# A transformer layer on one core: global q statistics in pairs with four square places, ropes on VectorE, and a curved schedule for the modulation products

## The chip, the cores and the metric

The kernel runs on one core of a Trainium2 chip. The metric is the device time of one execution in microseconds; three executions of the kernel before were timed. The profile is one further execution, recorded by the hardware profiler.

## The reference

One layer of a hybrid diffusion backbone: 1024 latent tokens of width 1024, 256 context tokens, float32. What matters here is the projection stage:

```
mod   = silu(c) @ w_mod + b_mod            # 6 x 1024 values: shift, scale, gate of mixer and FFN
mod_c = silu(c_ctx) @ w_mod[:, :2*1024] + ...   # the two that the context tokens need
h     = x   * (1 + scale1)  + shift1
h_c   = ctx * (1 + mod_c[1]) + mod_c[0]
proj  = h @ w_in + b_in                    # qa, ka, va, qb, kb, vb, gate logits (2 x 1024)
q_a   = rope(qa)                           # 8 heads of 64, windowed attention
q_b   = rope(rms(qb) * q_norm_g)           # 8 heads of 64, global attention
rms(t) = t * rsqrt(mean(t*t over the head) + 1e-6)
gates = sigmoid(gate logits)               # weights of the two branches
```

Behind it come the two attentions, their merge with the gates, a layer norm, a ConvFFN and a second layer norm.

## The kernel before

**Products in three parts.** Each float32 operand is split into a high part (a copy rounded to `fp32r`, line L82) and a low part (the difference, L87). `mm3` multiplies two operands with three matmuls: high by high (L90), high by low (L91), low by high (L92). A weight tile 128 x 512 is fetched into a raw tile (`raw`, 3 of them), then split into a pair of `wp` tiles (8, that is 4 pairs). In names, `w` is the raw tile, `wh` the high part, made on ScalarE, `wl` the low part, made on VectorE for the q and kv weights and on GpSimd for the gate weights (`wlg`).

**Order of TensorE's work.** First the global q (`q1`, names `accq1`, weights `wqb` of `in_w_qb`): 8 k tiles of the contraction x 8 token tiles x 3 matmuls, with the sums in all eight PSUM banks. While it runs, the tokens are modulated into `hT` (`hh`, `hl`). Then the program goes through a written list, `order`, made from `GORD = 3, 4, 4, 1, 4`: 3 gate tiles, `qa` (8 steps k), 4 gates, `qb` (8 steps), 4 gates, `ka` (8 steps), 1 gate, `kb` (8 steps), 4 gates. Here `qa` and `qb` are the windowed branch's q for token tiles 0-3 and 4-7 (both with the weights of `in_w_qa`; the names `wqa`/`wqb`, `accqa`/`accqb` follow the group), and `ka`, `kb` are keys and values with the context tokens, `cx`. A gate tile has two halves of 24 matmuls each; a step of `qa` or `qb` has 12. The loads of each step are issued ahead by `prefetch`: 2 or 4 steps early, as the 8 `wp` tiles allow.

**Modulation products.** 48 columns of the modulation matrix are wanted beside this work (16 for the context, 32 for the latent tokens' other factors). The list `late` holds them, and `mods(us)` is called behind each step with the number of matmuls of it. Each product takes a slot of the rotation of 19 large tiles (`ht`, H0 to H18, 128 x 1024, first put back is first taken), fetches a row block `wml` of 512 KB on SP's queue (L650) and multiplies and sums it on VectorE (`mod`, L188). So the rate follows the TensorE work done: `span[0]/span[1]` is the share of the matmuls up to the end of `ka` (840) that has been issued, and before the change the number of products issued is that share of 48:

```
        for _ in range(min(int(total * span[0] / span[1] + 0.01) - n, len(late))):
```

The slot is put back at once, so the next user of it waits for the product. The tiles `Q` (pairs of token tiles of a q) and the gates `sg` (until `late` is empty) take slots of the same rotation.

**The queue of side work.** `queue` holds for every token tile the steps behind its evacuation (`q_evac`, bias added while PSUM is read: VectorE, L301 for the global q, L299 for `qa`/`qb`). `side_step` takes one entry (in the slow mode every second time) and runs its first step; the remaining ones run at the next calls. For a global q tile, `qpost(1, t)` has a step `s1` (the rope table with the norm's gain folded in, by GpSimd; squares on ScalarE, L282, into one of two places `sqq`; sum per head on VectorE, L285; scaling and eps on VectorE, L286; power -1/2 on GpSimd, L287; the negative on GpSimd), an empty step, and `s2`: the rope (`rope`, L263 to L271: a product with the cosines, two half products with the sines, a sum), which goes to GpSimd for t = 2 and 5 and to VectorE else. The result of `s1` is read in attention. For `qa` and `qb` tiles `qpost(0, t)` holds only a rope.

**What sets the order.** Every engine and every DMA queue carries out its instructions in the order of the program. SP issues nearly all loads, so a load whose tile is not free holds the loads behind it. ScalarE's stream holds the high parts of the weights, the squares, the scaling of the context tiles `cx` (L632/L633, which need modulation columns 0 to 15) and the sigmoids of the gates with the issue of their stores (L668/L669); VectorE's holds the low parts, products, evacuations, statistics and ropes.

Of the kernel before, what the change touches and what calls it, by code (L numbers as in the profile page):

```python
# [7 lines left out]
F32 = mybir.dt.float32  # L8
R32 = mybir.dt.float32r
AF = mybir.ActivationFunctionType  # L10
ALU = mybir.AluOpType
AX = mybir.AxisListType

P = 128
# [4 lines left out]
NT = 8  # L19
HD = 64  # L20
# [5 lines left out]
QK_EPS = 1e-6  # L26
# [36 lines left out]
VOFF = 0.0  # L63
VSPAN = 1.0
VSC = 0, 1
DNS = {u0 + 2 * n + (u0 == 20): (n, j0, j1) for u0, j0, j1 in ((16, 0, 4), (20, 4, 8), (24, 8, 11)) for n in range(3)}


@with_exitstack
def layer_kernel(  # L70
# [6 lines left out]
    nc = tc.nc  # L77
# [18 lines left out]
    def ctile(shape, dt, name):  # L96
        return const.tile(shape, dt, tag=name, name=name)
# [15 lines left out]
    pqs, nqs = (cvt[:, n * 64:n * 64 + 64].rearrange("p (a b) -> p a b", b=8) for n in (0, 1))  # L113
    onec = ctile([P, 1], F32, "onec")
    onesf = ctile([P, P], F32, "onesf")
    mhalf = ctile([P, 8], F32, "mhalf")
    nc.vector.memset(onec, 1.0)
    nc.vector.memset(onesf, 1.0)
    nc.vector.memset(mhalf, -0.5)
# [13 lines left out]
    def ht(name, shape=(P, T), dt=F32):  # L133
        hslot[name] = pool, tag = hfree.pop(0)
        return pool.tile(list(shape), dt, tag=tag, name=name, bufs=1)

    def hput(*names):
        for n in names:
            hfree.append(hslot.pop(n))
# [5 lines left out]
    ph1 = tc.alloc_tile_pool(name="ph1", bufs=1, side="right", reuse_waits="tile")  # L145
# [9 lines left out]
    def pw(name, shape=(P, 512), dt=F32):  # L155
        return ph1.tile(list(shape), dt, tag="pw", name=name, bufs=PWB)
# [10 lines left out]
    def bias_tile(src, nm):  # L167
        b = ph1.tile([P, 512], F32, tag="bias", name=nm, bufs=2)
        nc.sync.dma_start(b, src.partition_broadcast(P))
        return b  # L170
# [11 lines left out]
    def tmp(name):  # L182
        t = ht(name)
        hput(name)
        return t

    def mod(w, row, bias, o):
        nc.vector.tensor_tensor_reduce(out=w, in0=w, in1=row, scale=1.0, scalar=bias, op0=ALU.mult, op1=ALU.add,  # L188
                                       accum_out=o)

    hT = []
    Q = {}
# [64 lines left out]
    def bc(ap, H):  # L257
        return ap.unsqueeze(1).to_broadcast([P, H, HD])

    def rope(eng, dst, src, H, cs, sn, nm, t1=None, t2=None):  # L260
        if t1 is None:
            t1, t2 = pw(f"rt1{nm}"), pw(f"rt2{nm}")
        eng.tensor_tensor(out=t1.rearrange("p (h d) -> p h d", d=HD), in0=src.rearrange("p (h d) -> p h d", d=HD),  # L263
                          in1=bc(cs, H), op=ALU.mult)
        sv = src.rearrange("p (h r a f) -> p h r a f", r=2, a=2, f=16)
        tv = t2.rearrange("p (h r a f) -> p h r a f", r=2, a=2, f=16)
        sg = sn.rearrange("p (r a f) -> p r a f", r=2, a=2)
        for a in (0, 1):
            eng.tensor_tensor(out=tv[:, :, :, a, :], in0=sv[:, :, :, 1 - a, :],
                              in1=sg[:, :, a, :].unsqueeze(1).to_broadcast([P, H, 2, 16]), op=ALU.mult)  # L270
        eng.tensor_tensor(out=dst, in0=t1, in1=t2, op=ALU.add)  # L271

    def gfold(dst, gi, t, eng):
        eng.tensor_tensor(out=dst[:, 0], in0=ropec[:, t], in1=gcol[:, gi], op=ALU.mult)
        sv = ropes[:, t].rearrange("p (r a f) -> p r a f", r=2, a=2)
        gv = gcol[:, gi].rearrange("p (r a f) -> p r a f", r=2, a=2)
        dv = dst[:, 1].rearrange("p (r a f) -> p r a f", r=2, a=2)
        for a in (0, 1):
            eng.tensor_tensor(out=dv[:, :, a, :], in0=sv[:, :, a, :], in1=gv[:, :, 1 - a, :], op=ALU.mult)

    def rms_scale(x3, H, nm, sq, ss=None):
        nc.scalar.activation(sq.rearrange("p (h d) -> p h d", d=HD), x3, AF.Square)  # L282
        if ss is None:
            ss = ph1.tile([P, 8], F32, tag="ss", name=f"ss{nm}", bufs=4)[:, 0:H]
        nc.vector.tensor_reduce(out=ss, in_=sq.rearrange("p (h d) -> p h d", d=HD), axis=AX.X, op=ALU.add)  # L285
        nc.vector.tensor_scalar(out=ss, in0=ss, scalar1=1.0 / HD, scalar2=QK_EPS, op0=ALU.mult, op1=ALU.add)  # L286
        nc.gpsimd.tensor_tensor(out=ss, in0=ss, in1=mhalf[:, 0:H], op=ALU.pow)  # L287
        return ss
# [4 lines left out]
    def q_evac(br, t, acc, bias):  # L293
        if t % 2 == 0:
            Q[br, t] = ht(f"Q{br}_{t}", (P, 2, 512))
        qq = Q[br, t - t % 2]
        q = qq[:, t % 2]
        if br == 0:
            nc.vector.scalar_tensor_tensor(out=q, in0=acc, scalar=0.125, in1=bias, op0=ALU.mult, op1=ALU.add)  # L299
        else:  # L300
            nc.vector.tensor_tensor(out=q, in0=acc, in1=bias, op=ALU.add)  # L301

    def qtile(br, t):
        return Q[br, t - t % 2][:, t % 2]

    def qpost(br, t):
        q = qtile(br, t)
        q3 = q.rearrange("p (h d) -> p h d", d=HD)
        if br == 0:
            def r0():  # L310
                rope(nc.gpsimd if t % 3 == 2 else nc.vector, q, q, 8, ropec[:, t], ropes[:, t], f"q0_{t}")
            return [r0]
        st = {}

        def s1():
            st["tb"] = ph1.tile([P, 2, HD], F32, tag="tb", name=f"tbq{t}", bufs=4)
            gfold(st["tb"], 0, t, nc.gpsimd)
            rms_scale(q3, 8, f"q{t}", sqq[0][:, t % 2], pqs[:, t])
            if t == NT - 1:
                sqq.clear()  # L320
                hput("sqq")
            nc.gpsimd.tensor_scalar(out=nqs[:, t], in0=pqs[:, t], scalar1=-1.0, scalar2=0.0, op0=ALU.mult, op1=ALU.add)

        def s2():
            tb = st["tb"]
            rope(nc.gpsimd if t % 3 == 2 else nc.vector, q, q, 8, tb[:, 0], tb[:, 1], f"q1_{t}")
        return [s1] + [lambda: None] * GAP + [s2]

    sqq = [ht("sqq", (P, 2, 512))]
    bias_qb = bias_tile(b_qb, "bias_qb")  # L330
    for t in range(NT):
        q_evac(1, t, acc[t], bias_qb)

    KL, KC, VT = [], [], []

    def kv_alloc():
        KL.extend(ht(f"KL{h}", dt=R32) for h in range(4))
        KC.append(ht("KC", (P, 4, NC), R32))
        VT.extend(ht(f"VT{t}", (P, 2, 4, P), R32) for t in range(5))
# [249 lines left out]
    def wd_sums(n, j0, j1):  # L589
        def a(r, c):  # L590
            return w_dn[c * NH + j0:c * NH + j1][:, :, 4 * r:4 * r + 4].rearrange("n p f q -> p n (f q)")

        def put(key, src, *more):
            tag = tokens.pop()
            t = dpool.tile([P, j1 - j0, HALF], F32, tag=tag, name=f"sd{key}_{j0}")
            for j in range(j0, j1):
                sd[key, j] = t[:, j - j0]
            sd[key] = t
            nc.sync.dma_start(t, src)
            for m in more:  # L600
                nc.gpsimd.dma_start(t, m, accum_op=ALU.add)

        if n == 0:
            put(1, a(1, 0), a(1, 1))
            put(3, a(0, 0), a(1, 0))
        elif n == 1:
            put(2, sd[1], a(0, 0))
        else:
            put(4, sd[2], a(0, 1))
# [28 lines left out]
    late = [(col, scc, modx[:, col:col + 1]) for col in range(16)]  # L638
    late += [(col, sc, modc[:, col:col + 1]) for col in range(16, 48)]

    total = len(late)
    span = [0.0, 0.0]

    def mods(us):
        span[0] += us
        n = total - len(late)
        for _ in range(min(int(total * span[0] / span[1] + 0.01) - n, len(late))):
            col, row, o = late.pop(0)
            w = tmp(f"wml{len(late)}")
            nc.sync.dma_start(w, wmodT[col])  # L650
            mod(w, row, bmc[:, col:col + 1], o)
            if not late:
                hput("sc", "scc")
                kv_alloc()
# [46 lines left out]
    for n, (gi, k) in enumerate(order):  # L701
# [9 lines left out]
        nm, src, tiles = groups[gi]  # L711
# [4 lines left out]
        for t in tiles:  # L716
            if t < NT:
                s = slice(t * P, (t + 1) * P)
                a = hT[k][0][:, s], hT[k][1][:, s]
            else:  # L720
                s = slice((t - NT) * P, (t - NT + 1) * P)
                a = c[0][:, s], c[1][:, s]
            mm3(acc[t], a, w, k == 0, k == KT - 1)
        mods(3 * len(tiles))
        if k == KT - 1:
            for t in tiles:
# [106 lines left out]
    for u in range(nu + 1):  # L833
# [3 lines left out]
        ss = []  # L837
        if u < nu:
            ss = units[u].score_steps()
# [11 lines left out]
        if u < nu:  # L851
            ss = [units[u].context] + ss
# [4 lines left out]
        for _, st_ in sorted(seq, key=lambda e: e[0]):  # L857
            st_()
        if u in DNS:
            wd_sums(*DNS[u])  # L860
        if u < nu:
# [82 lines left out]
    for f in range(2, KT):  # L944
# [4 lines left out]
        for j in range(4):  # L949
            k = (f % 2) * 4 + j  # L950
            for hf in (0, 1):
                a = O[1, hf, 0, j // 2][:, j % 2], O[1, hf, 1, j // 2][:, j % 2]
# [234 lines left out]
    for f in (4, 6):  # L1187
        for si in (1, 2):
# [3 lines left out]
            elif f == 6:  # L1192
                second = ln1(2)
                a = [n for n in range(len(pend)) if len(pend) - n <= KT]
# [122 lines left out]
    for k in range(4):  # L1317
        steps = build(k)
        n = 2 if k < 2 else 0
# [234 lines left out]
    nm = post.tile([P, nt], F32, tag="bnm", name="bnm")  # L1554
# [58 lines left out]
    for n in OTO:  # L1613
        t, a = n
# [122 lines left out]
```

## Time and profile before

| | |
|---|---|
| median of 3 runs | 1587.97 us (1587.14 to 1588.69) |
| span of the profiled execution | 1585.4 us |
| own time of the profiled execution | not given beside its span |
| TensorE (PE) busy | 1528.4 us, 96% |
| VectorE (DVE) busy | 1195.6 us, 75% |
| ScalarE (ACT) busy | 813.0 us, 51% |
| GpSimd (POOL) busy | 753.7 us, 48% |

The profile's page lists the busy time of each engine, the span in 40 slices with the granted TensorE clock and the DMA traffic, the chain of work that ended last, and groups of instructions: line, engine, operation, output <- inputs, count, then busy time, mean of one in ns, and the idle time of the engine just ahead of them with what ended it. A timeline row gives start and length in us, engine, line, operation and tiles; in square brackets stands the idle time of the engine ahead of the instruction and who ended it, and `x4` at the end means four instructions in a row taken together. The stage that the change touches lies between 16 and 345 us of the span.

### The profile page before, as it was taken

What the parts mean: (1) busy time and instruction counts of PE and PEld (TensorE: products, weight loads), DVE (VectorE), ACT (ScalarE), POOL (GpSimd) and SP (SyncE); (2) the same over time, 40 slices, a digit from 0 to 9 for tenths busy, and PEclk for the clock granted to TensorE, in tenths of its full rate; (3) what the DMA queues carried; (4) which work ended last, traced back from release to release, by engine and by line L of the source; (5) the groups of instructions that cost most, each with busy time, mean ns of one, the idle gap of its engine ahead of it and who ended that gap; (6) DMA issues with size and microseconds to landing.
All of it is one profiled execution on the core that took longest, in us unless ns stands there. A gap on an engine that the chain in (4) does not pass through costs nothing.

```text
span 1585.4 us, 22064 instructions
## 1 busy us (share of the span) xinstructions
PE 1528.4 (96%) x7680; PEld 1269.8 (80%) x7680; DVE 1195.6 (75%) x1766; ACT 813.0 (51%) x1443; POOL 753.7 (48%) x731
## 2 busy tenths in 40 slices
PE   6999999999999999999999999999999999999996
PEld 5878788878887887777788898888888888888876
DVE  7797646628888777888674779888888877657886
ACT  5422222448887667688531565444444444435642
POOL 0574302426667556665422554666667764021132
PEclk9999999999999999999999999999999999999998
DMA  9695662322236555531451132333334446996721
GB/s 378 217 313 188 221 217 81 120 80 67 62 104 157 139 127 145 118 73 39 142 186 53 60 101 86 114 107 112 115 106 118 111 113 189 358 273 210 255 94 53
DMA packets 112367, 229.98 MB, mean 145 GB/s; under 512 B 12960, under 2 KB 27808, under 8 KB 112160
## 3 DMA queue, kind: packets, MB, share of 16 engines
q1 hardware_dynamic: 96816, 198.93, 37.6%
q0 software_dynamic: 10400, 20.19, 8.2%
q10 hardware_dynamic: 5040, 9.46, 1.6%
q8 instruction: 60, 0.98, 0.3%
q14 instruction: 51, 0.42, 0.1%
HBM read 177.35 MB, written 65.86 MB: 153 GB/s over the span
## 4 chain that ended last, share of the span: by engine, by line
PE 82%; DVE 6%; ACT 4%; issue 3%; POOL 2%; DMA 2%; ACTq 0%; SPq 0%; DVEq 0%; POOLq 0%
PE ptr L531 5%; PE p L90 4%; PE p L91 4%; PE p L92 4%; PE g L90 3%; PE g L91 3%; PE g L92 3%; PE b L92 3%; PE b L91 3%; PE b L90 3%; PE s L414 2%; PE a L92 2%; PE c L91 2%; PE d L91 2%; PE c L92 2%
## 5 line engine op out<-in xcount | busy, mean ns | idle before, releaser
L541 DVE TENSOR_TENSOR ptl<-ptr,pth 128x512 fp32r<-128x512 f32 x188 | 124.8, 685 | 27.5 <-ACT pth L540 25.2
L531 PE MATMUL ptr<-ident,p 128*128 128x128 f32 x816 | 126.5, 278 | 10.3 <-DVE ptl L541 7.8
L540 ACT CAST pth<-ptr 128x512 fp32r<-128x512 f32 x188 | 106.6, 588 | 56.3 <-PE ptr L531 32.7
L87 DVE TENSOR_TENSOR ld<-rd,hd 128x1024 fp32r<-128x1024 f32 x77 | 94.0, 1240 | 52.5 <-ACT hd L82 50.4
L426 ACT ACTIVATE p<-p,nm 128x1024 f32<-128x1024 f32 (+2 forms) x128 | 125.3, 981 | 10.9 <-DVE p L459 10.1
L531 PEld LDWEIGHTS ptr<-ident,p 128*128 128x128 f32 x816 | 93.8, 140 | 40.3 <-DVE ptl L541 13.5
L82 ACT CAST hd<-rd 128x1024 fp32r<-128x1024 f32 x77 | 79.2, 1050 | 81.5 <-PE p L92 50.0
L552 PE MATMUL av<-pth,VT 128*128 128x512 f32 x236 | 104.6, 443 | 1.0 <-ACT avs L558 0.5
L90 PE MATMUL p<-hd 128*128 128x512 f32 x264 | 103.2, 391 | 0.0
L92 PE MATMUL p<-hd,ld 128*128 128x512 f32 x264 | 102.7, 389 | 0.0
L91 PE MATMUL p<-ld,hd 128*128 128x512 f32 x264 | 102.7, 389 | 0.0
L90 PE MATMUL g<-hh,whg 128*128 128x512 f32 x256 | 99.9, 390 | 0.0
L92 PE MATMUL g<-hh,wlg 128*128 128x512 f32 x256 | 99.7, 389 | 0.0
L91 PE MATMUL g<-hl,whg 128*128 128x512 f32 x256 | 99.6, 389 | 0.0
L553 PE MATMUL av<-ptl,VT 128*128 128x512 f32 x236 | 97.6, 414 | 2.0 <-POOL ptl L87 1.9
L87 POOL TENSOR_TENSOR wlg<-wg,whg 128x512 fp32r<-128x512 f32 x32 | 47.0, 1479 | 109.6 <-ACT whg L82 107.3
L459 DVE TENSOR_SCALAR_CACHE_REDUCE p<-s,cvt,nmc 128x1024 f32<-128x1024 f32 x64 | 84.5, 1340 | 12.3 <-PE s L415 11.8
L414 PE MATMUL s<-KL,q 128*128 128x512 f32 (+2 forms) x192 | 76.0, 396 | 2.9 <-ACT p_x L426 2.0
L188 DVE CUSTOM_DVE_ANT_0 wml<-wml,sc,bmc 128x1024 f32<-128x1024 f32 x32 | 45.0, 1416 | 39.0 <-DMA wml<-in_wmodT_dram 38.6
L84 POOL TENSOR_SCALAR pth<-prw 128x512 fp32r<-128x512 f32 x48 | 31.1, 649 | 88.2 <-ACT prw L537 62.7
L82 ACT CAST wS<-s 128x512 fp32r<-128x512 f32 x76 | 45.3, 621 | 52.1 <-POOL s L1079 51.3
L415 PE MATMUL s<-KL,q 128*128 128x512 f32 (+2 forms) x192 | 71.7, 373 | 0.0
(396 smaller groups left out, 4974.0 us busy)
## 6 DMA issues: line engine op xcount, KB each, us to landing
wml<-in_wmodT_dram SPq DMA_DIRECT2D x48, 512.0 KB
ru<-in_w_up_dram SPq DMA_DIRECT2D x38, 512.0 KB
rd<-td SPq DMA_DIRECT2D x55, 256.0 KB
rd<-sd SPq DMA_DIRECT2D x44, 256.0 KB
rd<-in_w_dn_dram SPq DMA_DIRECT2D x33, 256.0 KB
wm<-in_wmodT_dram SPq DMA_DIRECT2D x16, 512.0 KB
wg<-in_w_g_dram SPq DMA_DIRECT2D x32, 256.0 KB
sgd<-sg ACTq DMA_DIRECT2D x32, 256.0 KB
```

What stands on the lines that cost most here:

```text
L82: nc.scalar.copy(hi, src)
L87: lo_eng.tensor_tensor(out=lo, in0=src, in1=hi.bitcast(F32), op=ALU.subtract)
L90: nc.tensor.matmul(ps, a[0], b[0], start=start, stop=False, skip_group_check=resumed)
L91: nc.tensor.matmul(ps, a[0], b[1], start=False, stop=False, skip_group_check=resumed)
L92: nc.tensor.matmul(ps, a[1], b[0], start=False, stop=stop, skip_group_check=resumed)
L414: nc.tensor.matmul(o, self.q[0][:, hs], ks, start=True, stop=False)
L426: nc.scalar.activation(p, s, AF.Exp, bias=nm[:, h:h + 1], scale=scale, accum_out=sm[:, h:h + 1])
L531: nc.tensor.transpose(tr[:, h * P:(h + 1) * P], self.pslice(h, n), ident)
L540: nc.scalar.copy(hi, tr)
L541: nc.vector.tensor_tensor(out=lo, in0=tr, in1=hi.bitcast(F32), op=ALU.subtract)
L552: nc.tensor.matmul(self.av, v, hi, start=first, stop=False)
L553: nc.tensor.matmul(self.av, v, lo, start=False, stop=self.left == 0)
```

## The change

- The squares of the global q have two tiles `sqq0`, `sqq1` of two places each instead of one such tile. One ScalarE instruction squares two token tiles (128 x 1024). The first two are issued beside the evacuation (behind tiles 1 and 3), the other two behind the sum that empties their tile.
- The statistics run for two tiles at a time (`qstats`), in the step `s1` of the even tiles: one sum (VectorE), one scaling (VectorE), one power and one negative (GpSimd) over 16 columns instead of two each over 8; `mhalf` is 16 wide for it.
- All eight ropes of the global q run on VectorE.
- The number of modulation products issued follows x (0.4 + 0.6 x) of 48, where x is the share of matmuls, instead of x. Both curves start at 0 and end at 48 at the end of `ka`.
- The two square tiles hold one slot of the rotation more than before, until the last statistics.

```diff
+MOD0 = 0.4
...
-    mhalf = ctile([P, 8], F32, "mhalf")
+    mhalf = ctile([P, 16], F32, "mhalf")
...
         def s1():
             st["tb"] = ph1.tile([P, 2, HD], F32, tag="tb", name=f"tbq{t}", bufs=4)
             gfold(st["tb"], 0, t, nc.gpsimd)
-            rms_scale(q3, 8, f"q{t}", sqq[0][:, t % 2], pqs[:, t])
-            if t == NT - 1:
-                sqq.clear()
-                hput("sqq")
-            nc.gpsimd.tensor_scalar(out=nqs[:, t], in0=pqs[:, t], scalar1=-1.0, scalar2=0.0, op0=ALU.mult, op1=ALU.add)
+            if t % 2 == 0:
+                qstats(t)
...
-            rope(nc.gpsimd if t % 3 == 2 else nc.vector, q, q, 8, tb[:, 0], tb[:, 1], f"q1_{t}")
+            rope(nc.vector, q, q, 8, tb[:, 0], tb[:, 1], f"q1_{t}")
...
-    sqq = [ht("sqq", (P, 2, 512))]
+    sqq = [ht(f"sqq{n}", (P, 2, 512)) for n in (0, 1)]
+
+    def qsquare(t):
+        nc.scalar.activation(sqq[t // 2 % 2].rearrange("p a b -> p (a b)"), Q[1, t].rearrange("p a b -> p (a b)"),
+                             AF.Square)
+
+    def qstats(t):
+        sq = sqq[t // 2 % 2]
+        ss, ns = (a[:, t:t + 2].rearrange("p a b -> p (a b)") for a in (pqs, nqs))
+        nc.vector.tensor_reduce(out=ss, in_=sq.rearrange("p a (h d) -> p (a h) d", d=HD), axis=AX.X, op=ALU.add)
+        if t + 4 < NT:
+            qsquare(t + 4)
+        nc.vector.tensor_scalar(out=ss, in0=ss, scalar1=1.0 / HD, scalar2=QK_EPS, op0=ALU.mult, op1=ALU.add)
+        nc.gpsimd.tensor_tensor(out=ss, in0=ss, in1=mhalf, op=ALU.pow)
+        nc.gpsimd.tensor_scalar(out=ns, in0=ss, scalar1=-1.0, scalar2=0.0, op0=ALU.mult, op1=ALU.add)
+        if t + 2 == NT:
+            hput("sqq0", "sqq1")
+
     for t in range(NT):
         q_evac(1, t, acc[t], bias_qb)
+        if t in (1, 3):
+            qsquare(t - 1)
...
     def mods(us):
         span[0] += us
         n = total - len(late)
-        for _ in range(min(int(total * span[0] / span[1] + 0.01) - n, len(late))):
+        x = span[0] / span[1]
+        for _ in range(min(int(total * x * (MOD0 + (1 - MOD0) * x) + 0.01) - n, len(late))):
             col, row, o = late.pop(0)
             w = tmp(f"wml{len(late)}")
             nc.sync.dma_start(w, wmodT[col])
```

More of the change, by code (lines that the diff above doesn't have):

```diff
@@ L279, in gfold, with rms_scale @@
             eng.tensor_tensor(out=dv[:, :, a, :], in0=sv[:, :, a, :], in1=gv[:, :, 1 - a, :], op=ALU.mult)
-    def rms_scale(x3, H, nm, sq, ss=None):
+    def rms_scale(x3, H, nm, sq):
         nc.scalar.activation(sq.rearrange("p (h d) -> p h d", d=HD), x3, AF.Square)
-        if ss is None:
-            ss = ph1.tile([P, 8], F32, tag="ss", name=f"ss{nm}", bufs=4)[:, 0:H]
+        ss = ph1.tile([P, 8], F32, tag="ss", name=f"ss{nm}", bufs=4)[:, 0:H]
         nc.vector.tensor_reduce(out=ss, in_=sq.rearrange("p (h d) -> p h d", d=HD), axis=AX.X, op=ALU.add)
```

## The prediction

> **What bounds the kernel now.** I read the page's busy line first, then TensorE's waits in the projection stage that the change touches (16 to 345 us), then the timeline of that stage.
>
> ```profile
> span 1585.4 us, 22064 instructions
> PE 1528.4 (96%) x7680; PEld 1269.8 (80%) x7680; DVE 1195.6 (75%) x1766; ACT 813.0 (51%) x1443; POOL 753.7 (48%) x731
> ```
>
> TensorE is busy 96% of the span, so the edit can only win back idle TensorE time or add some. Its waits in this stage (total us, times, longest):
>
> ```profile
> PE accqa L91 <- DVE wlqa L87: 2.4, 1, 2.4
> PE accqb L91 <- DVE wlqb L87: 0.9, 1, 0.9
> PE accqa L90 <- ACT whqa L82: 0.7, 1, 0.7
> ```
>
> Three waits matter. Each is a weight split (`wlqa`, `wlqb` on VectorE, `whqa` on ScalarE) that comes late. TensorE's timeline (start, length) shows their price:
>
> ```profile
> 91.30 0.39 PE L90 MATMUL accqa<-whqa,hh 128*128 128x512 f32 x1
> 97.62 0.50 PE L90 MATMUL accqa<-whqa,hh 128*128 128x512 f32 x1 [0.71 <-ACT whqa L82]
> 100.52 0.79 PE L91 MATMUL accqa<-wlqa,hh 128*128 128x512 f32 x1 [2.40 <-DVE wlqa L87]
> 162.97 0.39 PE L90 MATMUL accqb<-whqb,hh 128*128 128x512 f32 x1
> 170.45 0.39 PE L90 MATMUL accqb<-whqb,hh 128*128 128x512 f32 x1
> 178.25 0.50 PE L91 MATMUL accqb<-wlqb,hh 128*128 128x512 f32 x1 [0.86 <-DVE wlqb L87]
> 186.31 0.39 PE L90 MATMUL g<-hh,whg 128*128 128x512 f32 x1
> ```
>
> 162.97 and 170.45 are 33 matmuls apart: 0.2267 us each. From 91.30 to 162.97 lie 288 matmuls (96 of qa, 192 of four gates): 65.29 us clean against 71.67, so 6.38 us are lost there. From 162.97 to 186.31 lie qb's 96: 21.76 against 23.34, 1.58 lost. Only 3.11 of the 6.38 is waiting. The rest is the clock. In the next table, by stretches of 5 us, stand the busy times of PE, PEld, DVE, ACT and POOL, then the granted clock, the DMA share and GB/s:
>
> ```profile
> 95.00:100.00 5.00, 2.40 (x10) 1.43 (x8) 5.00 (x7) 2.86 (x5) 4.92 (x5) 0.95 0.86 316
> 100.00:105.00 5.00, 4.48 (x11) 3.52 (x12) 5.00 (x9) 0.40 (x1) 4.14 (x3) 0.50 0.90 283
> 105.00:110.00 5.00, 5.00 (x21) 4.04 (x20) 5.00 (x11) 0.84 (x2) 1.74 (x3) 0.87 0.96 310
> 115.00:120.00 5.00, 5.00 (x24) 4.14 (x23) 5.00 (x10) 1.14 (x2) 1.76 (x1) 1.00 0.98 319
> ```
>
> The clock falls to 0.50 behind the 3.11 us gap, which costs 6.38 - 3.11 = 3.27 us more; the 0.86 us gap in qb costs no clock. VectorE is busy 5.00 of 5.00 us in all four rows: it is what is late in qa. In qb it is something else, which the chain of waits in that window names (start, length):
>
> ```profile
> 154.28 4.68 DMA wml<-in_wmodT_dram
> 159.09 1.28 DVE wml L188
> 160.42 3.62 DMA wml<-in_wmodT_dram
> 164.16 1.21 DVE wml L188
> 165.49 3.40 DMA wml<-in_wmodT_dram
> 171.32 4.84 DMA wml<-in_wmodT_dram
> 177.59 0.62 DVE wlqb L87
> 178.25 0.50 PE accqb L91
> ```
>
> Here a modulation row is fetched, multiplied, and only then is its slot free for the next fetch: rounds of 6.14, 5.07 and 5.83 us (154.28, 160.42, 165.49, 171.32). SP issues in order, so `wqb` loads stand behind a fetch that waits for a slot, and `wlqb` stands behind the products on VectorE. This chain is already as late as TensorE.
>
> **Part 1, statistics, squares and ropes: the qa stage.**
>
> ```profile
> L188 DVE CUSTOM_DVE_ANT_0 wml<-wml,scc,bmc 128x1024 f32<-128x1024 f32 x16 | 22.5, 1412 | 4.6 <-DMA wml<-in_wmodT_dram 4.5
> L269 DVE TENSOR_TENSOR rt2q<-Q,tbq 128x256 f32<-128x256 f32 x12 | 5.8, 508 | 0.0
> L285 DVE TENSOR_REDUCE cvt<-sqq 128x8 f32<-128x512 f32 x8 | 5.4, 675 | 0.0
> L271 DVE TENSOR_TENSOR Q<-rt1q,rt2q 128x512 f32<-128x512 f32 x6 | 4.6, 764 | 0.0
> L263 DVE TENSOR_TENSOR rt1q<-Q,tbq 128x512 f32<-128x512 f32 x6 | 4.1, 682 | 0.0
> L286 DVE TENSOR_SCALAR cvt<-cvt 128x8 f32<-128x8 f32 x8 | 3.0, 378 | 0.0
> L271 POOL TENSOR_TENSOR Q<-rt1q,rt2q 128x512 f32<-128x512 f32 x2 | 4.4, 2205 | 0.2
> L287 POOL TENSOR_TENSOR cvt<-cvt,mhalf 128x8 f32<-128x8 f32 x8 | 18.4, 2300 | 7.4 <-DVE cvt L286 7.4
> L287 POOL TENSOR_TENSOR ssk<-ssk,mhalf 128x2 f32<-128x2 f32 x10 | 8.2, 820 | 6.9 <-DVE ssk L286 6.5
> L282 ACT ACTIVATE sqq<-Q 128x512 f32<-128x512 f32 x8 | 5.0, 631 | 29.2 <-DVE cvt L285 21.8 <-DVE Q L301 7.4
> ```
>
> Two ropes come to VectorE: 2 x (0.68 + 2 x 0.51 + 0.76) = +4.9 us. Eight reductions become four of twice the size, between 0.68 and 1.35 us each; I take 1.35, no gain. Four small scalings go: -1.5. The curve moves products out: ahead of qa's evacuation VectorE had 24 of them and now has 16, 8 x 1.41 = -11.3. Sum -7.9 us. Ahead of the third `wlqa` (98.72 to 100.46 below; TensorE asks at 91.30 + 25 x 0.2267 = 97.0) the balance is smaller: 13 products become 9, -5.6, and the ropes of tiles 2 and 5 both lie there, +4.9; two scalings go, -0.8; the split itself may take 0.62 as in the chain above, not 1.74, -1.1, as GpSimd's ropes (2.2 us an add), which I read as what slowed it, are gone; half of the 4.5 us of late fetches goes, -2.2. In all -4.8: it is done at 95.6, 1.4 us before TensorE asks. The ends are nothing gained and the whole 6.38; I take the whole, since ScalarE's 21.8 us of waiting for a free square place, with `whqa` queued behind, goes too. GpSimd's power over 16 columns lies between 2.3 and 4.6 us; the line through 0.82 (2 columns) and 2.30 (8) gives 4.3. Only attention reads it, so it is free; without that cover it would cost 2 us a pair. At the start the first square waits for a second evacuation (a quarter of the 2.47 us for four below, 0.6), ahead of the first gate's `whg` on ScalarE: 0 to 0.6 us, I take 0.
>
> **Part 2, the curve: the qb stage.** The products that left qa have to be done by ka's end, and the program's own order puts 26 of them between the evacuations of qa and qb, where there were 14. Their fetches use each other's slots one after another.
>
> ```profile
> 59.47 2.14 DVE L188 CUSTOM_DVE_ANT_0 wml<-wml,scc,bmc 128x1024 f32<-128x1024 f32 x1
> 98.72 1.74 DVE L87 TENSOR_TENSOR wlqa<-wqa,whqa 128x512 fp32r<-128x512 f32 x1
> 125.92 2.47 DVE L299 SCALAR_TENSOR_TENSOR Q<-accqa,bias_qa 128x512 f32<-128x512 f32 x4
> 138.25 2.31 DVE L188 CUSTOM_DVE_ANT_0 wml<-wml,sc,bmc 128x1024 f32<-128x1024 f32 x1
> wml<-in_wmodT_dram SPq DMA_DIRECT2D x48, 512.0 KB
> wqb<-in_w_qa_dram SPq DMA_DIRECT2D x8, 256.0 KB
> ```
>
> Evacuation of qa: not before TensorE's end of it, 91.30 + 96 x 0.2267 = 113.1, and at the latest as now less the gain, 125.92 - 6.38 = 119.5; I take the middle, 116.3. The first product behind it and qa's ropes starts 12.33 us later (138.25 - 125.92) and lasts 1.3: 129.9. From there the new order makes six rounds before the third `wlqb`: rows 4 and 36 free the slot of 30; 34 that of 26; 26 that of 21; 21 that of 16; 16 is followed by the second `wlqb`, whose raw tile the fifth `wqb` load needs, which stands ahead of row 13 on SP; and rows 13 and 27 stand ahead of the third `wlqb`. By the shortest round (5.07), plus 1.3 in the first two for a second product and 0.6 for a split in the fifth, and 3.74 + 2 x 1.3 + 0.6 for the last, that is 6.4 + 6.4 + 5.1 + 5.1 + 5.7 + 6.9 = 35.6 us, so 165.5. TensorE now starts qb at 162.97 - 6.38 = 156.6 and asks for that split 25 matmuls later, at 162.3: a stall of 3.2 us. But 15 rows of 512 KB, 6 weight loads and 5 gate stores of 256 KB each in 35.6 us are 300 GB/s, and the DMAs gave 319 at a share of 0.98. So the rounds will be of the crowded kind; between the mean of the three (5.68) and the longest (6.14) I take 5.9, 0.83 more in each of six: 5.0. The stall is 8.2 us, and a gap over 3 us drew the slow clock, 3.27.
>
> The Trainium skill (DMA: Bandwidth & Descriptors, Anatomy of one DMA) fits a GpSimd-issued transfer as 2.0 us plus bytes over 436 GB/s. As an estimate that is 3.2 us for 512 KB, against 3.74 from issue to product here; six such rounds would be 3.2 us shorter, and the time 1588.3.
>
> **Sum** against the profiled span of 1585.4 us; the page gives no time of its own for that execution, so I lay the same 2.6 us around it that separate the span from the median of the runs, 1587.97. qa -6.38, qb's old loss -1.58, new stall +8.2, its clock +3.27: +3.5 us, **1591.5**. All later stages have the same instructions and come out later as a whole.
>
> **Rivals.**
> *The chain of rounds stays hidden* (not slower). VectorE is early enough that evacuation starts at 113.1, and rounds are the shortest: 113.1 + 13.6 + 35.6 = 162.3, just when TensorE asks. Then both losses vanish: 1587.97 - 7.96 = 1580.0. For it: VectorE is 11 us less loaded, and GpSimd no longer disturbs it. Against: it needs both lower ends at once, in a stage whose fetch chain is on the critical chain already with 14 rows. A stall of up to 3 us without the clock still gives 1583. The point where it decides is the third `wlqb` at 162.3.
> *qa still stalls.* On ScalarE the new order puts a context tile's scaling, which needs row 38, ahead of the third `whqa`. If row 38 lands 5 us late, the old gap and its clock stay and the second stage shifts with it, with less of a stall there: 1594 to 1598.
> *The scheduler evens it out*: fewer stalls in qa, as many in qb, within 1 us of before.
> A rule of the skill (TensorE: Matmul & The Clock Gate, the table of the last part) lets the clock drop only after a gap of about 3 us or more; by it the 3.2 us stall of short rounds could keep the clock. Here two gaps of 0.71 and 2.40 were enough, so I keep the charge.
>
> **Chances.** New stall 0.62 (own range 1586.5, short rounds, to 1596, evacuation at 119.5 and rounds of 6.1), hidden 0.22, qa stalls too 0.11, evened out 0.05. About 0.2%, 3.2 us, is what a measurement can tell from no change. Of the first case 0.70 lies above that, 0.25 within, 0.05 below. Slower 0.62 x 0.70 + 0.11 = 0.54; same 0.155 + 0.05 = 0.21; faster 0.03 + 0.22 = 0.25. The range 1581 to 1597 leaves out the best of the hidden case and the worst of the rest.
>
> **What would show it.** Right: no wait for `wlqa` in TensorE's list, a wait of 3 to 10 us for `wlqb` near 162, the granted clock at 0.5 behind it and 1.0 from 95 to 110, fetches of `wml` in the chain from 130 on. Wrong: no `wlqb` wait over 2 us (the rounds were hidden), or the gap at 97 still there.

## The result, and the profile after

The changed kernel takes 1609.52 us (median of 4 runs, 1607.01 to 1611.23) against 1588.03 us before: a ratio of 1.0131, 95% interval 1.0119 to 1.0143, 21.5 us slower. The forecast was 3.5 us slower, in a range that ended at 1597. The sign was right, the size was not.

The head of the page, of the changed kernel:

```profile
span 1605.9 us, 22053 instructions
PE 1544.1 (96%) x7680; PEld 1269.2 (79%) x7680; DVE 1199.8 (75%) x1766; ACT 812.1 (51%) x1439; POOL 739.3 (46%) x715
```

The span grew by 20.5 us and TensorE's busy time by 15.7 of them, with the same 7680 matmuls. That is the first sign that waits are not the main loss. TensorE's one wait on a weight in the projection stage (us, times, longest), and the rows of its timeline that bound the stages:

```profile
PE accqb L92 <- DVE wlqb L88: 9.7, 2, 5.0
```

```profile
91.19 0.39 PE L91 MATMUL accqa<-whqa,hh 128*128 128x512 f32 x1
...
156.75 0.39 PE L91 MATMUL accqb<-whqb,hh 128*128 128x512 f32 x1
162.11 0.79 PE L92 MATMUL accqb<-wlqb,hh 128*128 128x512 f32 x1 [4.98 <-DVE wlqb L88]
...
174.97 0.80 PE L92 MATMUL accqb<-wlqb,hh 128*128 128x512 f32 x1 [4.73 <-DVE wlqb L88]
...
194.00 0.39 PE L91 MATMUL g<-hh,whg 128*128 128x512 f32 x1
```

The reader is to see three lengths. From 91.19 to 156.75 are 65.56 us, 0.27 more than 288 matmuls need: the old loss of 6.38 is gone. From 156.75 to 194.00 are 37.25 us for 96 matmuls that need 21.76: 15.49 lost, where before lost 1.58. From 194.00 to the end are 1411.9 us, against 1399.1 from 186.31 before: 12.8 us lost in stages whose instructions did not change.

The 15.49 us are 9.71 of waiting and 5.78 of slow clock. Windows (us; busy PE, PEld, DVE, ACT, POOL; clock, DMA share, GB/s):

```profile
160.00:165.00 5.00, 2.89 (x7) 2.31 (x8) 3.84 (x6) 0.00 (x0) 0.00 (x0) 0.54 0.97 333
165.00:170.00 5.00, 5.00 (x19) 3.88 (x17) 3.65 (x7) 1.73 (x3) 0.00 (x0) 0.77 0.80 298
175.00:180.00 5.00, 5.00 (x12) 3.98 (x13) 4.52 (x8) 0.62 (x1) 0.00 (x0) 0.50 0.92 265
```

Each of the two gaps drew its own slow stretch. For the 12.8 us behind them, one window of the ConvFFN, of before and then of the changed kernel:

```profile
1100.00:1200.00 100.00, 100.00 (x443) 82.81 (x442) 86.50 (x78) 49.35 (x69) 69.59 (x39) 1.00 0.35 106
```

```profile
1100.00:1200.00 100.00, 100.00 (x432) 80.90 (x431) 85.85 (x77) 47.20 (x67) 68.48 (x37) 1.00 0.33 106
```

TensorE is busy for all 100 us in both, waits for nothing, and its granted clock reads 1.00 in both. Yet 432 matmuls lie in the window in place of 443. The pitch, the time from the start of one matmul to the start of the next, is 0.2320 us there instead of 0.2267. Taken over 100 us each, it stays between 0.231 and 0.232 from about 800 us on, and every kind of 512-column matmul there is slower, whatever it multiplies. In attention, from 345 to 800 us, the mean pitch of these matmuls was 0.230 to 0.231 us already before, and is 0.233 in the changed kernel.

### The profile page after: what moved, and what is told of

Its sections match the earlier page's. It is cut to its first block, busy times and chain, and to the rows that moved or that the text cites. A ratio compares the mean times of both kernels' runs of the same rounds, so it can differ in the third digit from the quotient of the medians.

```text
span 1605.9 us, 22053 instructions
## 1 busy us (share of the span) xinstructions
PE 1544.1 (96%) x7680; PEld 1269.2 (79%) x7680; DVE 1199.8 (75%) x1766; ACT 812.1 (51%) x1439; POOL 739.3 (46%) x715
## 4 chain that ended last, share of the span: by engine, by line
PE 77%; DVE 9%; ACT 4%; DMA 4%; issue 3%; POOL 2%; ACTq 0%; SPq 0%; DVEq 0%; POOLq 0%
PE ptr L547 5%; PE p L93 4%; PE p L91 4%; PE p L92 4%; DMA wml<-in_wmodT_dram 3%; PE b L93 3%; PE b L92 3%; PE b L91 3%; PE d L91 2%; PE d L92 2%; PE c L91 2%; PE s L430 2%; PE a L93 2%; PE c L92 2%; PE a L91 2%
## 5 line engine op out<-in xcount | busy, mean ns | idle before, releaser
L91 PE MATMUL g<-hh,whg 128*128 128x512 f32 x256 | 99.9, 390 | 0.0
L83 ACT CAST wA<-ru 128x512 fp32r<-128x512 f32 x57 | 35.5, 622 | 68.5 <-PE d L93 38.0
```

Source lines behind the costliest of these rows:

```text
L83: nc.scalar.copy(hi, src)
L91: nc.tensor.matmul(ps, a[0], b[0], start=start, stop=False, skip_group_check=resumed)
```

## The experiments

Four questions: what slows the late matmuls, which part of the change costs what, what sets the waits of the second group, and what won the first group. Ratios are against the kernel before, run on the same chip, with 95% intervals.

### The late pitch

**e1_layout**, **e4_after_layout**: the 19 slots renamed.

```diff
-    hfree = [(hp, f"H{n}") for n in range(19)]
+    hfree = [(hp, f"H{n}") for n in (0, 1, 2, 9, 13, 14, 10, 12, 11, 4, 6, 7, 5, 3, 15, 16, 17, 18, 8)]
```

The list shown is that of e1, before with the changed kernel's placing; e4 has the inverse in the changed kernel.

> The kernel before, with the 19 slots of the rotation renamed so that every tile from attention on lies where it lies in the changed kernel; the order of all work is that of before. In the changed kernel the matmuls of 512 columns run at a pitch of 0.2320 us from about 800 us on, where before has 0.2267 (some 12 of the 21.5 us). Theory 'place': it is where the tiles lie; then the pitch is 0.232 here too and the time near 1588 + 12 = 1600 us, with no stall at the second windowed q group beyond the old 0.9 us. Theory 'history': it comes from the stalls of the projection stage and the slow clock behind them; then the time stays at 1588, within 2 us, and the pitch at 0.2267.

> The changed kernel, with the slots renamed so that from attention on every tile lies where it lies in the kernel before. 'Place': the pitch goes back to 0.2267, and only the early loss is left, about 8 us: 1596 to 1598. 'History': 1609 as the changed kernel, pitch 0.232. In both the two waits for the low weight parts of the second windowed q group stay, about 5 us each.

e1: 1587.89 us, ratio 0.9994 (0.9985 to 1.0003). e4: 1610.35, ratio 1.0136 (1.0121 to 1.0151). Which slot a tile lies in does not matter. That left "history", and it fell with the parts of the change run alone.

**e2_stats** (the changed kernel with `MOD0 = 1.0`) and **e3_curve** (before with the curve alone).

> The changed kernel with the old straight line of products (MOD0 = 1): statistics in pairs and ropes on VectorE alone. Theory 'chain of rounds': the two waits of 5 us for the second windowed q group go (below 1.5 us together), and the first group's third low part, with its 13 products ahead again and 4.9 us of ropes more, is as late as before, about 3 us of waits and 3 us of slow clock; time 1587 to 1590 if the late pitch comes from the 5 us stalls, 1599 to 1602 if it comes from the places of the tiles. Rival 'VectorE is too full': waits of some 5 us for the second group stay, time above 1595 even at the old pitch.

> The kernel before with the growing curve alone (0.4). 'Chain of rounds': the waits of 4 to 5 us for the second windowed q group come as in the changed kernel, the first group's waits go, and the offset behind that stage is +6 to +9 us; with the late pitch of the changed kernel the time is 1605 to 1610, without it 1594 to 1597. Rival 'VectorE is too full (ropes)': the waits at the second group stay under 2 us and the time is at or below 1585.

e2: 1607.86 us, 1.0116 (1.0100 to 1.0133). e3: 1594.91, 1.0039 (1.0026 to 1.0052). The curve alone has its stall of 6.78 us with the slow clock behind it, but its late pitch is 0.2267: stalls do not cause the late loss. The statistics alone have the pitch of 0.2320. Nothing in them runs after 345 us, but one line of them moves memory: the constant of -0.5 grew from 8 to 16 columns, 32 bytes, and everything allocated behind it on the lower side (the 19 slots, attention outputs, later pools) begins 32 bytes further up. The tiles that are allocated from the top (weights of the late stages and others) stay.

**e5_before_m16**: the kernel before with that one number.

```diff
-    mhalf = ctile([P, 8], F32, "mhalf")
+    mhalf = ctile([P, 16], F32, "mhalf")
```

> The kernel before with one number changed: the constant tile of -0.5 is 16 columns wide, as in the changed kernel, of which 8 are used. Every instruction is that of before; all tiles that lie behind it on the same side of the memory (the 19 slots, later the attention outputs) begin 32 bytes further up. Theory 'bytes': the late pitch of 0.2320 us comes from where these tiles begin: time 1588 + 12 to 14 = 1600 to 1602 us, the projection stage as before. Rival 'statistics': the pitch comes from something that the paired statistics or the ropes do; time 1588, pitch 0.2267.

1604.48 us (1600.58 to 1610.64), 1.0098 (1.0071 to 1.0125). Eight columns that nobody reads cost some 15 us, by the interval 11 to 20. The window of e5:

```profile
1100.00:1200.00 100.00, 100.00 (x432) 80.88 (x432) 85.85 (x77) 46.95 (x68) 68.59 (x37) 1.00 0.34 106
```

**e6_after_m24**, **e7_after_m40**: the changed kernel with the same constant 24 or 40 wide, 16 used: the lower side 64 or 128 bytes up. **e9_stats_m40**: as e7, with `MOD0 = 1.0` (the straight line) too.

> The changed kernel with the constant 24 columns wide, 16 used: the tiles begin 64 bytes further up than before. 'Bytes', counted in steps of 64: pitch 0.2267 and 1596 to 1597 us; 'bytes' in steps of 128: the pitch stays above 0.2267 and the time near 1609. 'Statistics': 1609.

> The changed kernel with the constant 40 columns wide, 16 used: the tiles begin 128 bytes further up than before. 'Bytes' (64 or 128): the 12.9 us that the changed kernel loses behind 800 us go, pitch 0.2267, time 1609.5 - 12.9 = 1596.6; the 9.7 us of waits for the second windowed q group stay. 'Statistics': 1609.

> The paired statistics and the ropes on VectorE with the old straight line of products (MOD0 = 1), and the tiles 128 bytes up as in the kernel with 40 columns. 'Bytes': without the late growth (21.7 - 7.1 = 14.6 us in the run with 16 columns) 1607.9 - 14.6 = 1593.3. The waits of the projection stage are those of the run with 16 columns, 9.3 us for the second group. If its early loss of 7 us came from the bytes too (the products and evacuations read and write these tiles), the time is 1582 to 1588.

e6: 1609.88 us, 1.0131 (1.0116 to 1.0146). e7: 1608.62, 1.0117 (1.0100 to 1.0134). e9: 1604.78, 1.0097 (1.0082 to 1.0112). The late pitch was 0.231 to 0.233 in each, so neither 64 nor 128 bytes is the step: the gains that "bytes" promised at 64 or 128 did not come. The times of e6 (as by steps of 128 too) and e7 are those of the rival "statistics", which e5 contradicts, as it is slow with the old statistics. The next four ask what the step refers to.

**f4_both_down32**: before, `negsink` (32 bytes) allocated on the upper side, so both sides begin 32 bytes lower. **f5_right_down64**: before, 64 unused bytes at the top, so the upper side alone begins 64 bytes lower. **f1_after_m8**: the changed kernel with the old constant. **g4_before_up256**: before, the lower side 256 bytes up, with two kinds of small attention tiles in two buffers instead of four to make room.

```diff
 f1, against the changed kernel:
-    mhalf = ctile([P, 16], F32, "mhalf")
+    mhalf = ctile([P, 8], F32, "mhalf")
...
-        nc.gpsimd.tensor_tensor(out=ss, in0=ss, in1=mhalf, op=ALU.pow)
+        for a in (0, 1):
+            nc.gpsimd.tensor_tensor(out=pqs[:, t + a], in0=pqs[:, t + a], in1=mhalf, op=ALU.pow)
 g4, against before:
-    mhalf = ctile([P, 8], F32, "mhalf")
+    mhalf = ctile([P, 72], F32, "mhalf")
...
-                        bufs=4)
+                        bufs=2 if name[:3] in ("nmc", "smc") else 4)
```

> The kernel before with one small constant (32 bytes) moved from the lower to the upper side of the memory: the tiles of both sides begin 32 bytes further down, so that their distance from each other stays and their places change. Theory 'distance': the pitch depends on the places of the two sides relative to each other; it stays at 0.2267 and the time at 1588. Theory 'place': the slots have to begin at one particular offset; the pitch is 0.231 to 0.233 and the time 1600.

> The kernel before with 64 unused bytes at the top of the upper side: the tiles of the upper side begin 64 bytes further down, the slots of the lower side stay. 'Distance': the late pitch becomes 0.231 to 0.233 and the time 1600 or more. 'Place of the slots': 0.2267 and 1588. What the early stage, whose matmul operands lie on the upper side alone, does with the shift is open; its pitch should stay at 0.2267 by 'distance'.

> The changed kernel with the constant of -0.5 back at 8 columns (the power is taken in two instructions of 8 columns on GpSimd instead of one of 16), so that all tiles begin where they begin in the kernel before. 'Bytes': the late pitch goes back to 0.2267 and the 12.9 us with it: 1609.5 - 12.9 = 1596.6, range 1595 to 1599, with the two waits of 5 us for the second windowed q group as in the changed kernel. If the pitch stays at 0.232, the statistics do something that the widths of tiles do not explain.

> The kernel before with the tiles of the lower side 256 bytes further up; to make room two kinds of small tiles of the attention have two buffers instead of four. Shifts of the two sides against each other by 32, 64 and 128 bytes made the late pitch 0.231 to 0.233. If the distance counts modulo 256, the pitch is 0.2267 and the time 1588 to 1590; if not, 1600 or more.

f4: 1588.91 us, 1.0001 (0.9990 to 1.0012). f5: 1603.39, 1.0088 (1.0070 to 1.0106). f1: 1593.59, 1.0035 (1.0022 to 1.0049). g4: 1588.54, 1.0002 (0.9989 to 1.0015). The same window of f4, f5, f1 and g4, in this order:

```profile
1100.00:1200.00 100.00, 100.00 (x442) 82.79 (x442) 86.49 (x77) 48.84 (x68) 68.91 (x40) 1.00 0.35 106
```

```profile
1100.00:1200.00 100.00, 100.00 (x434) 81.04 (x433) 84.00 (x77) 47.15 (x67) 68.84 (x38) 1.00 0.35 109
```

```profile
1100.00:1200.00 100.00, 100.00 (x443) 82.81 (x442) 86.28 (x81) 47.82 (x68) 66.14 (x38) 1.00 0.36 112
```

```profile
1100.00:1200.00 100.00, 100.00 (x443) 82.81 (x442) 86.50 (x78) 49.46 (x69) 69.43 (x39) 1.00 0.35 106
```

Moving both sides together costs nothing, moving either against the other by 32, 64 or 128 bytes costs the pitch, 256 bytes cost nothing. f1 has the paired statistics and the old pitch, e5 the old statistics and the slow one, so it is the bytes and not the statistics. And it is the distance of the two sides, modulo 256 bytes as far as tried (256 is the only multiple). In the kernel before they agree, by the addresses in its program: the slots begin at 19680 and the late weights at 147424, both 224 over a multiple of 256. The 32 bytes (e5, 1.0098) and the rest of the change (f1, 1.0035) multiply to 1.0133, against the 1.0131 measured for the whole; so close a match is partly luck, as e5's interval alone is 0.0027 wide on each side.

### The waits of the second group

f1 is the change as it was meant, and it is 4.9 us slower than before on its chip (ratio 0.22 to 0.49% above 1, that is 3.5 to 7.8 us): the forecast of 3.5 lies at the edge. Its profiled execution took 1596.82 us, 3.2 above the median, so the waits in its list may be above the usual:

```profile
PE accqb L92 <- DVE wlqb L88: 10.6, 2, 6.2
```

The parts alone lose too. TensorE's waits of e9 (statistics and ropes, straight line; e2's are alike, 9.3 us for `wlqb`) and of e3 (curve alone):

```profile
PE accqb L92 <- DVE wlqb L88: 7.1, 3, 3.1
PE g L91 <- ACT whg L83: 1.4, 1, 1.4
```

```profile
PE accqb L92 <- DVE wlqb L88: 8.7, 3, 6.8
PE accqa L92 <- DVE wlqa L88: 1.7, 2, 1.5
PE accqa L91 <- ACT whqa L83: 0.7, 1, 0.7
```

In e9 and e2 the first group's own 96 matmuls lost little (0.5 and 0.8 us, against 6.4 before and 4.8 in e3). The four gates behind it lost 2.6 and 2.7 us, which lost nothing before and 0.2 in the changed kernel. TensorE still came to the second group earlier than before, where the low parts were no earlier: the gain was given back, with a slow clock on top. I had expected e2's first group to stay late, by about 3 us and a slow clock, and its waits in the second below 1.5. Both were wrong, the second because I had priced that group's chain against TensorE's old arrival.

**f3_after_m8_vrope**: f1 with the ropes of the windowed q on VectorE alone.

```diff
-                rope(nc.gpsimd if t % 3 == 2 else nc.vector, q, q, 8, ropec[:, t], ropes[:, t], f"q0_{t}")
+                rope(nc.vector, q, q, 8, ropec[:, t], ropes[:, t], f"q0_{t}")
```

> As the kernel before it, and the ropes of the windowed q tiles on VectorE alone too. In the changed kernel VectorE stands 8.1 us (121.7 to 129.8) behind GpSimd's rope of the windowed q's third tile, whose scratch tiles it needs, between the evacuation of the first group and the first product. Theory 'chain of rounds': with that rope on VectorE (2.45 us) the chain starts 5.6 us earlier, the waits of 9.7 us fall to about 4 and one of the two slow clocks goes (3 us): 1588, range 1585 to 1592. Rival 'the DMA share is the limit' (0.9 to 1.0 between 150 and 185 us): starting earlier gains little, waits stay above 8 us, 1594 to 1597.

1592.66 us, 1.0026 (1.0015 to 1.0038): not told apart from f1, waits 9.9 us. The waits are those of the rival, the time is that of neither. My expectation misread the chain of waits. VectorE's timeline of the changed kernel:

```profile
117.63 2.15 DVE L189 CUSTOM_DVE_ANT_0 wml<-wml,sc,bmc 128x1024 f32<-128x1024 f32 x1 [4.49 <-DMA wml<-in_wmodT_dram]
...
119.71 2.47 DVE L299 SCALAR_TENSOR_TENSOR Q<-accqa,bias_qa 128x512 f32<-128x512 f32 x4
...
129.75 2.37 DVE L270 TENSOR_TENSOR rt2q<-Q,ropet 128x256 f32<-128x256 f32 x2 [1.21 <-POOL Q L272]
132.05 2.31 DVE L189 CUSTOM_DVE_ANT_0 wml<-wml,sc,bmc 128x1024 f32<-128x1024 f32 x1
```

VectorE stood only 1.21 us for GpSimd's rope; the rest of the 12.34 us is its own work. And the evacuation, which TensorE allows from 113, stands behind a product that waits 4.49 us for its row.

**g1_mod0**, **h2_mod2**, **g2_mod7**: f1 with `MOD0` 0.0, 0.2 and 0.7 in place of 0.4. **g3_before_mod0**: before with the curve at 0.0.

> The changed kernel with the constant at 8 columns (old places of the tiles), and the curve steeper: MOD0 = 0, the number of products is 48 x squared. By the formula 3 products are issued at the end of the first windowed q group and 12 at the start of the second, where 0.4 gives 7 and 17, and the straight line 13 and 24. Theory 'chain of rounds': with 0.4 VectorE did 17 products in the 45 us from 130.8 to 175.5, 2.6 us each; five fewer ahead of the second group are 13 us, more than its 10.6 us of waits. The waits go, the 6.4 us of the first group stay gained: 1588 - 8 = 1580, range 1579 to 1584, unless the 29 products left for the stage behind are late there. Rival 'the queue of loads': SP's order and the DMAs set the waits whatever the number; waits above 5 us, 1590 to 1595.

> The same kernel with MOD0 = 0.2, between 0 (1583.7 us, waits of 0.9 us for the second group) and 0.4 (1593.6 us, 10.6 us). 'Chain of rounds': 5 products at the end of the first group and 15 at the start of the second, against 3 and 12 or 7 and 17: waits of some 5 us, 1585 to 1591. If the waits come all at once where a load stands behind a full slot, they are those of one of the two ends.

> As the kernel before it with MOD0 = 0.7: 10 products at the end of the first windowed q group and 21 at the start of the second. 'Chain of rounds': four more ahead of the second group than with 0.4, up to 10 us later, but TensorE's clock and the earlier start of products in the first group give some of it back; waits of 10 to 15 us, 1595 to 1602. Rival 'the queue of loads': as with 0.4, 1593 to 1595.

> The kernel before (old statistics, two square places, ropes of tiles 2 and 5 on GpSimd) with the curve of MOD0 = 0. 'Chain of rounds': the second group's waits go below 2 us; the first group's stay to the part that the squares cause (with 0.4: 2.4 us): 1582 to 1586. If the paired statistics are what the gain needs, it stays at 1587 to 1590.

g1: 1583.67 us, 0.9973 (0.9962 to 0.9983). h2: 1583.29, 0.9977 (0.9964 to 0.9990). g2: 1595.63, 1.0051 (1.0038 to 1.0064). g3: 1594.25, 1.0038 (1.0023 to 1.0052). Waits of g1, then h2, then g2:

```profile
PE acckb L91 <- DVE ch L87: 1.7, 1, 1.7
PE accqa L92 <- DVE wlqa L88: 1.4, 2, 1.2
PE accqb L92 <- DVE wlqb L88: 0.9, 1, 0.9
```

```profile
PE accqb L92 <- DVE wlqb L88: 2.0, 1, 2.0
```

```profile
PE accqb L92 <- DVE wlqb L88: 7.7, 4, 5.1
PE accqb L91 <- ACT whqb L83: 5.0, 1, 5.0
```

Fewer products ahead of the second group remove its waits, which the rival "queue of loads" excluded. Every product less is also a fetch less, and which of the two counts was not separated. The waits do not grow in proportion: 0.9, 2.0, 10.6 and 12.7 us (7.7 + 5.0) at 0, 0.2, 0.4 and 0.7, each from one profile, and h2 was faster than the 1585 to 1591 us expected of it. Both g1 and h2 are faster than the kernel before, by 4.7 and 4.8 us on their chips; they aren't told apart from each other. At 0 the 23 products left behind the second group show up in `kb` (1.7 us for a context split). g3, the old statistics and ropes with the same curve as g1, missed both of its ranges: it is slower than before. Its second group waits only 2.9 us, but its first is later than ever:

```profile
PE accqa L92 <- DVE wlqa L88: 6.7, 3, 6.1
```

### What won the first group

**h1_pool_ropes**: g1 with the global ropes of tiles 2 and 5 back on GpSimd.

```diff
-            rope(nc.vector, q, q, 8, tb[:, 0], tb[:, 1], f"q1_{t}")
+            rope(nc.gpsimd if t % 3 == 2 else nc.vector, q, q, 8, tb[:, 0], tb[:, 1], f"q1_{t}")
```

> The fastest kernel so far (paired statistics with the power in two halves, ropes on VectorE, MOD0 = 0) with the global ropes of tiles 2 and 5 back on GpSimd. It tells which part of the change the first windowed q group's gain needs: with the old statistics and the same curve its low parts were 6.7 us late, here 1.4. Theory 'GpSimd's ropes': they slow VectorE's work ahead of the third low part; the 6 us of waits come back, 1587 to 1593. Rival 'squares': the four square places and the pairs are what helps; waits stay below 2 us and the time at 1582 to 1585.

1592.43 us, 1.0024 (1.0014 to 1.0035), against 0.9973 for g1. Its waits on the first group, and VectorE's half rope products there (from 58 to 120 us: busy, mean ns, idle before and what ended it):

```profile
PE accqa L92 <- DVE wlqa L88: 3.1, 2, 2.0
PE accqa L91 <- ACT whqa L83: 2.6, 1, 2.6
```

```profile
L270 DVE TENSOR_TENSOR rt2q<-Q,tbq 128x256 f32<-128x256 f32 x12 | 4.7, 431 | 9.3 <-POOL Q L272 9.3
```

With GpSimd's two ropes back, VectorE stands 9.3 us for the scratch tiles (`pw`, five) that a rope on GpSimd holds, and the first group waits again, 5.7 us. With the slow clock it loses 9.4 us, as much as in g3 (9.1), which has the old statistics and square places. So the gain needs the ropes on VectorE, and the pairs and squares win nothing that shows while two ropes are on GpSimd; VectorE's ropes with the old statistics were not run. In the kernel before that idle time does not show (0.0), so that h1's wait is not what held its low parts back; what did is not shown by a run of its own.

## Why the prediction was right or wrong

**What bounds the kernel, and the first group: right in the result, not in the balance.** All 6.38 us were booked as gained, and 6.1 came (0.27 us lost now). The third low part was forecast done at 95.6 us. It was done at 94.38 in the changed kernel, and at 94.48 in e2, which has the straight line:

```profile
93.70 0.68 DVE L88 TENSOR_TENSOR wlqa<-wqa,whqa 128x512 fp32r<-128x512 f32 x1
```

```profile
93.80 0.68 DVE L88 TENSOR_TENSOR wlqa<-wqa,whqa 128x512 fp32r<-128x512 f32 x1
```

By the sum e2 should have been 4.2 us later, with 12 products of 1.41 us ahead of that split instead of 9. With the curve alone (e3) it was done at 99.9, against 100.46 before. So the ropes and statistics won the group itself, and not the products that the curve moved away, which the sum needed (5.6 us) to pay for two more ropes on VectorE (4.9). That it came out near the truth was luck. What the curve won lies in the four gates behind the group, where the straight line of e2 loses 2.7 us.

The prediction also read GpSimd's ropes as what slowed VectorE's work. Between 58 and 120 us, before and then after:

```profile
L87 DVE TENSOR_TENSOR wlqa<-wqa,whqa 128x512 fp32r<-128x512 f32 x8 | 7.6, 949 | 0.0
```

```profile
L88 DVE TENSOR_TENSOR wlqa<-wqa,whqa 128x512 fp32r<-128x512 f32 x8 | 5.4, 678 | 0.0
L338 DVE TENSOR_SCALAR cvt<-cvt 128x16 f32<-128x16 f32 x4 | 0.6, 160 | 0.0
L335 DVE TENSOR_REDUCE cvt<-sqq 128x16 f32<-128x1024 f32 x4 | 4.8, 1205 | 0.0
L339 POOL TENSOR_TENSOR cvt<-cvt,mhalf 128x16 f32<-128x16 f32 x4 | 14.0, 3512 | 9.1 <-DVE cvt L338 9.1
```

The split fell from 949 to 678 ns and the scaling from 378 ns to 160 on twice the columns. The scaling fits the reading in h1 too (711 ns with two ropes back on GpSimd), the split does not: 693 ns in h1, and 826 in h2, whose ropes are all on VectorE. The pair's sum took 1205 ns (booked 1.35 us), the power 3.5 us (line: 4.3), hidden as said.

**The second group: right in kind, 4 us short.** The third low part was forecast done at 165.5 + 5.0 = 170.5, and was done at 174.92:

```profile
174.24 0.68 DVE L88 TENSOR_TENSOR wlqb<-wqb,whqb 128x512 fp32r<-128x512 f32 x1
```

The six rounds, counted from the end of the first product (132.05 + 2.31 = 134.36) to there, took 40.6 us, just as booked. The 4.4 us that it came later lie ahead of the rounds, in the term that gave 129.9 for the end of that product. Of the ends 113.1 and 119.5 for the evacuation I took the middle, 116.3, and it was 119.71 (3.4 us), since it stands on VectorE behind a product that waits for its row; and the first product took 2.31 us where 1.3 was booked (1.0 us). The first low part, which the sum did not look at, was late as well (161.37), but by these rows that cost little: without its gap TensorE would have asked for the third at 156.75 + 25 x 0.2267 = 162.4 and waited until 174.97, 12.5 us. The slow clock behind that makes the rest, 2.9, of the 15.49 us lost, where 8.2 + 3.27 = 11.47 were booked.

**"All later stages have the same instructions and come out later as a whole": the step that failed.** The late stages did not come out as a whole: they took 12.8 us more, of the 20.5 in the span. I counted the wider constant as a longer power only, and not as 32 bytes in front of every slot. What the runs showed in its place is a pitch of 0.232 us instead of 0.2267 behind 800 us, from those 32 bytes alone (e5 with them, f1 without). None of the rivals had it, though the wider constant stood in the diff.

**The rivals.** "The chain of rounds stays hidden" did not come with 0.4; with 0 and 0.2 it nearly did, at 1583.7 and 1583.3, not 1580.0. "qa still stalls" did not come. The rule of the Trainium skill on gaps (TensorE: Matmul & The Clock Gate, the table of the last part) agrees with the changed kernel's gaps of 4.98 and 4.73 us, which both drew the slow clock.

A shorter gap was enough in other runs. In h2 a single gap of 1.97 us was followed by a granted clock of 0.66 in the next 5 us:

```profile
165.28 0.59 PE L92 MATMUL accqb<-wlqb,hh 128*128 128x512 f32 x1 [1.97 <-DVE wlqb L88]
165.00:170.00 5.00, 4.72 (x14) 3.72 (x15) 2.63 (x5) 1.16 (x2) 0.00 (x0) 0.66 0.66 193
```

In g1 a gap of 1.66 us ahead of 275.07 left it at 1.00. Where the border lies was not tried.

**Left open.** Why the distance of two sides acts on nearly all matmuls alike was not settled. By the addresses in the changed kernel's program, the late matmuls whose two operands both lie on the lower side also run slower, at 0.230 us, and those with both on the upper side at 0.232, against 0.227 for either before. So the distance between a matmul's own two operands is not the whole account. Nor does it explain attention, which runs at 0.230 to 0.231 us in the kernel before.

## What to carry to other kernels

Read a diff for what it allocates, not only for what it executes: a constant that grows by 32 bytes shifts every tile behind it, and here that cost about three times as much as the rest of the change (e5 against f1). Compare the start-to-start pitch of matmuls in stages that the change does not touch; busy share and granted clock do not show it. And a gain ahead of a chain of fetches is only worth what the next chain allows: price the next stage against the new arrival of TensorE. Run the parts of a change one by one, too: a sum can come out right with terms that are not.

## What the runs showed of the hardware

Between 900 and 1500 us, TensorE's pitch on 512 columns of fp32r, 0.2267 us, became 0.231 to 0.233 when the tiles of the two sides of the memory began at offsets that differ by 32, 64 or 128 bytes modulo 256, and was 0.2267 at 0 and at 256. The granted clock read 1.00 in all of them. The projection stage, whose matmul operands all lie on the upper side, kept 0.227 in each of them.
